# Gated attention's values turned by a round trip through DRAM and 32x32 transposes on VectorE, in place of TensorE transposes

## The chip, the cores and the metric

The kernel runs on one core of a Trainium2 chip. The time is that of one execution on the device, in microseconds (us), as the median of several runs. Five engines work side by side, each through its own list of instructions in a fixed order: TensorE (PE: matmuls, and transposes done as matmuls against an identity matrix), VectorE (DVE), ScalarE (ACT), GpSimd (POOL) and SyncE (SP, which here only starts transfers). An instruction waits on semaphores for those whose results or buffers it needs, and everything behind it on its engine waits with it. Matmul results go to PSUM, which has eight banks; all other tiles lie in SBUF.

## The reference

One decoder layer works on 256 tokens with 16 learned tokens put in front (272), at a model width of 2048, batch 1:

```
xn = rmsnorm(h);  proj = xn @ w_in
o_fox = forgetting_attention(...)            # 8 heads of width 128
g = log_sigmoid(ga @ w_alpha2 + b_alpha) / 16
o_gla = gated_linear_attention(gq, gk, gv, g) # 4 heads, keys 256, values 512 wide
o_gla = head_rmsnorm(o_gla) * silu(gr)
y = sigmoid(gate_fox) * (o_fox @ w_o_fox) + sigmoid(gate_gla) * (o_gla @ w_o_gla)
h = h + y @ w_out
h = h + squared_relu(rmsnorm(h) @ w_ff1) @ w_ff2
out = rmsnorm(h)[16:]
```

In gated linear attention every token's query and key are scaled by running products of the gates ("decay"); scores are the products of scaled queries and keys, masked to be causal, and a head's output is scores times values. The change concerns the four heads of this part alone.

## The kernel before, in words

Activations stay transposed: features on the 128 partitions, tokens on the free axis. All projections stream the weight matrices once, as chunks of 128 output columns. `next_weights` fetches a chunk as two halves of 512 KB: SP starts the transfer into `raw` (5 buffers), ACT rounds it to a high part (L128), DVE subtracts to get the low part (L129), both in one of 5 `wt` buffers. A new half can only be rounded when PE has finished with the half that was five before it. A chunk is then used by one of two products:

- `gemm2` (L144, L145): 32 matmuls on 256 tokens, its two column halves added later by `total` (ACT copies one half to `evb`, L170; DVE adds, `evt`, L173);
- `gemm_all` (L161 to L163): 48 matmuls on all 272 tokens.

Each such product writes one bank of the pool `pg`, which has three. So the fourth product from any given one needs the bank that this one filled, and can begin only when the engine that reads that result is done with it. Small results go through a pool `px` of five banks.

`later(n, fn)` puts a function aside until n more products have been issued. On top of that a scheduler settles each engine's order when the program is built; what runs in which order is fixed from then on.

A head of gated attention (`gla_head`) makes two key products (results scaled on DVE into `ki`, L511), two query products (L514), four value products, then four products for the output gate (`sg`). Head 0 has its queries and gates from earlier. Value product i is scaled by DVE into `vT` (first 256 tokens, L558) and `vE` (last 16, L559); with L559 the PSUM bank is free again. Since this gives values with features on partitions, and the output product wants tokens there, `turn` (L544 to L553) turns them: eight 128x128 TensorE transposes of `vT` and one of `vE` (L548 to L550), then the first 128 tokens are split into a high and a low part (`v0`, ACT L177 and DVE L178), the second 128 copied to `v1` (ACT L552), the last 16 to `v2` (ACT L553).

`scores` (L530) makes the masked scores `at0`, `at1`, `at2`. `outputs` multiplies them with the values into two `po` banks: twelve matmuls for the first block (L190 to L192), then those of the second (L574) and the last block (L575). ACT copies the result to `oT` (L576) and squares it into `so` (L577), POOL adds squares. `sums` adds over features (L585), and DVE forms the reciprocal root (L206 to L212). `scale` multiplies `oT` by it (L591) and by the gate (L593) and splits it (L178, into `og`). `decays` makes the gate products of the next head from DVE's scans (L436), with twelve ACT exponentials (L445, L451).

These steps of one head run among the products of the next: the root and the scaling of head 0 stand on DVE between the value products of head 1.

Of the kernel before, what the change touches and what calls it, by code (L numbers as in the profile page):

```python
# [7 lines left out]
F32 = mybir.dt.float32  # L8
# [4 lines left out]
ALU = mybir.AluOpType  # L13
# [3 lines left out]
P = 128  # L17
D = 2048
KT = D // P
NM = 16  # L20
NT = 256
# [3 lines left out]
GLA_H, GLA_DK, GLA_DV = 4, 256, 512  # L25
# [8 lines left out]
BIG = 3.0e38  # L34
RAW = 5
NL = 4

O_FQ, O_FK, O_FV, O_FF = 0, 1024, 2048, 3072
O_GQ, O_GK, O_GV, O_GR = 3080, 4104, 5128, 7176
# [29 lines left out]
def trunk(ctx: ExitStack, tc: tile.TileContext, hT, w_small, w_all, consts, w_alpha2, out):  # L69
    nc = tc.nc  # L70
    serial = [0]

    def nm(s):
        serial[0] += 1
        return f"{s}_{serial[0]}"
# [5 lines left out]
    dram = ctx.enter_context(tc.tile_pool(name="dram", bufs=1, space=bass.MemoryType.DRAM))  # L81
    pg = ctx.enter_context(tc.tile_pool(name="pg", bufs=3, space=PSUM))
    px = ctx.enter_context(tc.tile_pool(name="px", bufs=5, space=PSUM))
# [3 lines left out]
    def bank(pool, s):  # L87
        return pool.tile([P, 512], F32, tag="bank", name=nm(s))
# [5 lines left out]
    def later(n, fn):  # L94
        waiting.append([n, fn])
# [80 lines left out]
    def split_to(dst_hi, dst_lo, src):  # L176
        nc.scalar.copy(dst_hi, src)  # L177
        nc.vector.tensor_tensor(dst_lo, src, dst_hi.bitcast(F32), op=ALU.subtract)  # L178

    def split(pool, tag, src, bufs=None):  # L180

        kw = {} if bufs is None else {"bufs": bufs}
        hi = pool.tile(list(src.shape), F32R, tag=tag + "h", name=nm(tag + "h"), **kw)
        lo = pool.tile(list(src.shape), F32R, tag=tag + "l", name=nm(tag + "l"), **kw)
        split_to(hi, lo, src)
        return hi, lo

    def three(out, lhs, rhs, first, last):

        nc.tensor.matmul(out, lhs[0], rhs[0], start=first, stop=False)  # L190
        nc.tensor.matmul(out, lhs[0], rhs[1], start=False, stop=False)
        nc.tensor.matmul(out, lhs[1], rhs[0], start=False, stop=last)  # L192
# [60 lines left out]
    ident, scan = cons[:, 0:P], cons[:, P : P + NA]  # L253
# [79 lines left out]
    for s in range(KT // 2):  # L333
# [4 lines left out]
        for kk in range(2):  # L338
# [11 lines left out]
            st, sp = k == 0, k == KT - 1  # L350
            for c, (hi, lo) in enumerate(at):
                ps = first_ps[c]
# [5 lines left out]
            for c, (hi, lo) in enumerate(at):  # L358
                ps = first_ps[c]
# [28 lines left out]
    rb = keep.tile([P, NA], F32, tag="rb", name="rb")  # L388
# [113 lines left out]
    def gla_head(hd, sg, ready=None):  # L502

        ki = att.tile([P, 2, NA], F32, tag="ki", name=nm("ki"))
        q0 = ready[0] if ready else att.tile([P, 2, NT], F32, tag="qd", name=nm("qd"))
        q1 = att.tile([P, 2, NT - G1], F32, tag="q1", name=nm("q1"))
        q2 = att.tile([P, 2, NM], F32, tag="q2", name=nm("q2"))
        k2 = att.tile([P, 2, 4, NM], F32, tag="k2", name=nm("k2"))
        for i in range(2):
            ps = ready[1] if ready and i == 0 else gemm_all(next_weights(), x)  # L510
            nc.vector.tensor_tensor(ki[:, i, :], ps[:, 0:NA], rb, op=ALU.mult)  # L511
        for i in range(2):
            t = q0[:, i, :] if ready else total(gemm2(next_weights(), xt))
            nc.vector.scalar_tensor_tensor(q0[:, i, :], t, GLA_DK ** -0.5, rbt, op0=ALU.mult, op1=ALU.mult)  # L514
        e = decay[hd]
        nc.vector.tensor_tensor(ki, ki, e[:, :, Q:], op=ALU.mult)
        nc.vector.tensor_copy(k2, ki[:, :, 2 * P :].unsqueeze(2).to_broadcast([P, 2, 4, NM]))
        nc.vector.tensor_tensor(q1, q0[:, :, G1:], e[:, :, NT : Q - NM], op=ALU.mult)
        nc.vector.tensor_tensor(q2, q0[:, :, G2:], e[:, :, Q - NM : Q], op=ALU.mult)
        nc.vector.tensor_tensor(q0, q0, e[:, :, 0:NT], op=ALU.mult)  # L520

        at1 = att.tile([P, NT - G1], F32, tag="at1", name=nm("at1"))

        def scores():
            pa = bank(px, "pa")
            p0, p1, p2 = pa[:, 0:NT], pa[:, NT : 2 * NT - G1], pa[0 : 4 * NM, 2 * NT - G1 : Q]
            for dst, k, q in ((p0, ki[:, :, 0:P], q0), (p1, ki[:, :, P : 2 * P], q1),
                              (p2, k2.rearrange("p a j s -> p a (j s)"), q2)):
                for a in range(2):
                    nc.tensor.matmul(dst, k[:, a, :], q[:, a, :], start=(a == 0), stop=(a == 1))  # L530
            nc.scalar.copy(at0, p0)
            nc.scalar.copy(at1, p1)
            nc.vector.tensor_tensor(at2[0 : 4 * NM].rearrange("p (j q) -> p j q", q=NM),
                                    p2.unsqueeze(1).to_broadcast([4 * NM, 4, NM]),
                                    diag[0 : 4 * NM].rearrange("p (j q) -> p j q", q=NM), op=ALU.mult)
            for ap, n, base in ((at0[:, 0:G1], G1, NM), (at1[:, 0:P], P, 0)):
                nc.gpsimd.affine_select(ap, ap, pattern=[[1, n]], compare_op=ALU.is_ge, fill=0.0, base=base,
                                        channel_multiplier=-1)

        v1 = att.tile([P, GLA_DV], F32, tag="v1", name=nm("v1"))  # L540
        vT = att.tile([P, 4, 2 * P], F32, tag="vT", name=nm("vT"))
        vE = att.tile([P, 4 * NM], F32, tag="vE", name=nm("vE"))

        def turn():  # L544
            pv = [bank(px, n) for n in ("p0", "p1", "p2")]
            for i in range(4):
                cols = slice(P * i, P * (i + 1))
                nc.tensor.transpose(pv[0][:, cols], vT[:, i, 0:P], ident)  # L548
                nc.tensor.transpose(pv[1][:, cols], vT[:, i, P : 2 * P], ident)
            nc.tensor.transpose(pv[2][0 : 4 * NM, 0:P], vE, ident)  # L550
            split_to(*v0, pv[0])
            nc.scalar.copy(v1, pv[1])  # L552
            nc.scalar.copy(v2[0 : 4 * NM], pv[2][0 : 4 * NM, 0:P])  # L553

        later(5, scores)
        for i in range(4):
            ps = gemm_all(next_weights(), x)
            nc.vector.tensor_tensor(vT[:, i, :], ps[:, 0 : 2 * P], rb[:, 0 : 2 * P], op=ALU.mult)  # L558
            nc.vector.tensor_tensor(vE[:, NM * i : NM * (i + 1)], ps[:, 2 * P : NA], rb[:, 2 * P :], op=ALU.mult)  # L559
        later(1, turn)  # L560

        oT = att.tile([P, 4, NT], F32, tag="oT", name=nm("oT"))
        st = {}

        def outputs():
            a0 = split(att, "a0", at0)
            so = st["so"] = att.tile([P, 4, NT], F32, tag="vT", name=nm("so"))
            po = [bank(px, "po").rearrange("p (j t) -> p j t", t=NT) for _ in range(2)]
            for c in range(4):
                three(po[c // 2][:, c % 2, :], [e[:, P * c : P * (c + 1)] for e in v0], a0, c % 2 == 0, False)  # L570
            for i, pj in enumerate(po):
                for j in range(2):
                    v = slice(P * (2 * i + j), P * (2 * i + j + 1))
                    nc.tensor.matmul(pj[:, j, G1:], v1[:, v], at1, start=False, stop=False)  # L574
                nc.tensor.matmul(pj[:, :, G2:], v2, at2[:, 2 * NM * i : 2 * NM * (i + 1)], start=False, stop=True)  # L575
                nc.scalar.copy(oT[:, 2 * i : 2 * i + 2, :], pj)  # L576
                nc.scalar.activation(so[:, 2 * i : 2 * i + 2, :], pj, AF.Square)  # L577
            nc.gpsimd.tensor_tensor(so[:, 0:2, :], so[:, 0:2, :], so[:, 2:4, :], op=ALU.add)
            nc.gpsimd.tensor_tensor(so[:, 0, :], so[:, 0, :], so[:, 1, :], op=ALU.add)
            st["sq"] = split(att, "sq", so[:, 0, :])  # L580

        def sums():
            pr = bank(px, "pr")[:, 0:NT]
            for i in range(2):
                nc.tensor.matmul(pr, ones_r, st["sq"][i], start=(i == 0), stop=(i == 1))  # L585
            st["y"] = root(pr, NT, 1.0 / GLA_DV, [st["so"][:, i, :] for i in (1, 2, 3, 3)])

        def scale():
            for i in range(4):
                j = 4 * hd + i  # L590
                nc.vector.scalar_tensor_tensor(oT[:, i, :], oT[:, i, :], ggn[:, j : j + 1], st["y"], op0=ALU.mult,  # L591
                                               op1=ALU.mult)
                nc.vector.tensor_tensor(oT[:, i, :], oT[:, i, :], st["sg"][:, i, :], op=ALU.mult)  # L593
                split_to(og_tile()[j][:, 0, :], og_tile()[j][:, 1, :], oT[:, i, :])

        later(2, outputs)
        later(3, sums)
        if sg is None:
            sg = gla_gates(None)
            st["sg"] = sg  # L600
            scale()
        else:
            st["sg"] = sg
            later(8, scale)

    att = cum.enter_context(tc.tile_pool(name="att", bufs=1, reuse_waits="tile"))

# [375 lines left out]
```

## Time and profile before

| | |
|---|---|
| median of 3 runs | 1597.83 us (1597.78 to 1598.25) |
| profiled execution | 1597.77 us |
| its span, first to last instruction | 1595.8 us |
| mean granted TensorE clock | 0.998 of full speed |
| PE busy | 1585.7 us (99%) |
| DVE busy | 1056.4 us (66%) |
| ACT busy | 778.6 us (49%) |
| POOL busy | 90.4 us (6%) |
| DMA | 293.15 MB, mean 184 GB/s |

Busy times are sums over the whole span, and an engine that is busy for two thirds of it can still be late at one place. A timeline row gives start and length; matmuls and most other instructions overlap a little with their successors, so the pitch from one start to the next is what an instruction costs in a row of its kind. "Idle before" with an arrow names what ended the wait.

Gated attention's value products of head 0 lie at about 60 to 83 us, those of head 1 at about 115 to 138 us.

### The profile page before, as it was taken

The page shows a single profiled execution, that of the slowest core. Times are in us where ns is not written, and L with a number is a line of the kernel's source. Part 1 is how long each engine was busy: PE and PEld are TensorE (multiplying, and loading weights), DVE is VectorE, ACT ScalarE, POOL GpSimd, SP SyncE. Part 2 cuts the span into 40 slices and gives each one's busy share as a digit, 9 for nine tenths or more (in the row PEclk, how much of TensorE's full clock was granted, in tenths as well). Part 3 has the DMA queues.
Part 4 walks back from the last instruction along what each step waited for, and adds up shares of the span by engine and source line. Part 5 has one row for each costly group of instructions (what it writes and reads, how often), then busy time and mean ns, then how long its engine had stood idle before and what let it go on. Part 6 is the DMA issues. An engine that isn't in the chain of part 4 may idle for free.

```text
span 1595.8 us, 25249 instructions
## 1 busy us (share of the span) xinstructions
PE 1585.7 (99%) x9838; PEld 1437.4 (90%) x9838; DVE 1056.4 (66%) x1613; ACT 778.6 (49%) x1173; POOL 90.4 (6%) x139
## 2 busy tenths in 40 slices
PE   9999999999999999999999999999999999999997
PEld 8999999999998888888888888888888888888887
DVE  7777757675556666666777776667655776567655
ACT  7776444454445444444555444344433443344553
POOL 0000000011100000000011000000000000000011
PEclk9999999999999999999999999999999999999999
DMA  9444545455545555555555555555555555555552
GB/s 319 168 151 162 179 158 182 156 179 166 166 160 183 188 193 187 188 194 188 182 200 189 183 194 188 192 189 187 192 189 191 191 186 195 188 190 192 186 185 94
DMA packets 88392, 293.15 MB, mean 184 GB/s; under 512 B 9344, under 2 KB 18320, under 8 KB 88272
## 3 DMA queue, kind: packets, MB, share of 16 engines
q1 hardware_dynamic: 87104, 289.67, 54.2%
q0 software_dynamic: 448, 1.13, 0.4%
q8 instruction: 77, 1.26, 0.3%
q10 hardware_dynamic: 720, 0.74, 0.2%
q14 instruction: 43, 0.35, 0.1%
HBM read 289.39 MB, written 2.11 MB: 183 GB/s over the span
## 4 chain that ended last, share of the span: by engine, by line
PE 99%; DVE 0%; DMA 0%; ACT 0%; issue 0%; DVEq 0%; ACTq 0%
PE ps L144 50%; PE ps L145 27%; PE psa L163 5%; PE psa L162 5%; PE psa L161 5%; PE ps L354 1%; PE ps L876 1%; PE ps L361 1%; PE ps L863 0%; PE pa L530 0%; PE po L574 0%; PE psa L616 0%; DMA h<-hT_dram 0%; DVE scaled L908 0%; PE pq L683 0%; PE p L548 0%
## 5 line engine op out<-in xcount | busy, mean ns | idle before, releaser
L129 DVE TENSOR_TENSOR wt<-raw,wt 128x1024 fp32r<-128x1024 f32 x522 | 644.7, 1235 | 338.4 <-ACT wt L128 332.8
L128 ACT CAST wt<-raw 128x1024 fp32r<-128x1024 f32 x522 | 548.7, 1052 | 509.1 <-PE ps L145 277.4
L144 PE MATMUL ps<-x,wt 128*128 128x512 f32 x1952 | 680.5, 391 | 0.0
L145 PE MATMUL ps<-x,wt 128*128 128x256 f32 x1952 | 550.5, 282 | 0.0
L144 PEld LDWEIGHTS ps<-x,wt 128*128 128x128 f32 x1952 | 366.4, 188 | 75.8
L145 PEld LDWEIGHTS ps<-x,wt 128*128 128x128 f32 x1952 | 368.9, 189 | 0.2
L144 PE MATMUL ps<-a,wt 128*128 128x512 f32 x960 | 333.0, 390 | 0.0
L145 PE MATMUL ps<-a,wt 128*128 128x256 f32 x960 | 270.7, 282 | 0.0
L144 PEld LDWEIGHTS ps<-a,wt 128*128 128x128 f32 x960 | 180.1, 188 | 37.8
L161 PE MATMUL psa<-x,wt 128*128 128x272 f32 x624 | 181.7, 291 | 0.0
L145 PEld LDWEIGHTS ps<-a,wt 128*128 128x128 f32 x960 | 181.4, 189 | 0.0
L163 PE MATMUL psa<-x,wt 128*128 128x272 f32 x624 | 180.7, 290 | 0.0
L162 PE MATMUL psa<-x,wt 128*128 128x272 f32 x624 | 180.5, 289 | 0.0
L170 ACT COPY evb<-ps 128x256 f32<-128x256 f32 x160 | 59.4, 372 | 229.1 <-PE ps L145 227.2
L173 DVE TENSOR_TENSOR evt<-ps,evb 128x256 f32<-128x256 f32 x158 | 67.0, 425 | 99.0 <-ACT evb L170 98.8
L161 PEld LDWEIGHTS psa<-x,wt 128*128 128x128 f32 x624 | 117.2, 188 | 0.4
L162 PEld LDWEIGHTS psa<-x,wt 128*128 128x128 f32 x624 | 117.3, 188 | 0.0
L163 PEld LDWEIGHTS psa<-x,wt 128*128 128x128 f32 x624 | 117.2, 188 | 0.0
L144 PE MATMUL ps<-og,wt 128*128 128x512 f32 x256 | 89.2, 390 | 0.0
L144 PE MATMUL ps<-y,wt 128*128 128x512 f32 x256 | 88.8, 390 | 0.0
L145 PE MATMUL ps<-og,wt 128*128 128x256 f32 x256 | 72.2, 282 | 0.0
L145 PE MATMUL ps<-y,wt 128*128 128x256 f32 x256 | 72.2, 282 | 0.0
(281 smaller groups left out, 1317.9 us busy)
## 6 DMA issues: line engine op xcount, KB each, us to landing
raw<-w_all_dram SPq DMA_DIRECT2D x537, 512.0 KB, 3.6
raw<-w_all_dram SPq DMA_DIRECT2D x7, 384.0 KB, 5.7
h<-hT_dram SPq DMA_DIRECT2D x7, 275.0 KB, 6.1
out_dram<-scaled SPq DMA_DIRECT2D x5, 256.0 KB, 2.7
negc<-fdram POOLq DMA_DIRECT2D x8, 136.0 KB, 3.6
raw<-w_all_dram SPq DMA_DIRECT2D x2, 256.0 KB, 3.7
raw<-w_all_dram SPq DMA_DIRECT2D x2, 192.0 KB, 4.5
room<-w_small_dram SPq DMA_DIRECT2D x1, 320.0 KB, 6.4
```

What stands on the lines that cost most here:

```text
L128: nc.scalar.copy(hi[:, k, :], r)
L129: nc.vector.tensor_tensor(lo[:, k, :], r, hi[:, k, :].bitcast(F32), op=ALU.subtract)
L144: nc.tensor.matmul(ps, hi, x, start=first, stop=False)
L145: nc.tensor.matmul(ps[:, 0:NT], lo, x[:, 0, :], start=False, stop=last)
L161: nc.tensor.matmul(ps[:, 0:n], hi, x[:, k, 0, :], start=(k == 0), stop=False)
L162: nc.tensor.matmul(ps[:, 0:n], lo, x[:, k, 0, :], start=False, stop=False)
L163: nc.tensor.matmul(ps[:, 0:n], hi, x[:, k, 1, :], start=False, stop=(k == KT - 1))
L170: nc.scalar.copy(b, ps[:, NT:512])
L173: nc.vector.tensor_tensor(t, ps[:, 0:NT], b, op=ALU.add)
L354: nc.tensor.matmul(ps, hi, x[:, k, :, NM:NA], start=st, stop=False)
L361: nc.tensor.matmul(ps[:, 0:NT], lo, x[:, k, 0, NM:NA], start=False, stop=sp)
L876: pin(nc.tensor.matmul(ps[:, NT:], w(k)[0], a[k][:, :, tok], start=(k == 0), stop=(k == KT - 1)))
```

## The change

The eight TensorE transposes of `vT` per head go. `vT` is stored as 8 blocks of 32 tokens, each with the four value products side by side. `turn` sends it to a DRAM tile `rows` by one transfer (256 pieces of 2 KB), fetches it back by four transfers into `moved` (each fills 32 partitions, pieces of 512 B), and DVE then transposes it in 32x32 blocks with eight instructions of 128x128, four into `turned` and four into `v1`. All five transfers are started by POOL. `v0` is split from `turned`. ACT's copy to `v1` goes. The small transpose of `vE` stays on PE, as `turn_end`, called in `outputs` behind the twelve matmuls. `turn` is called directly behind the four value products instead of one product later; `outputs` and `sums` are each put aside one product longer, `scale` one less for heads 1 to 3. `moved` and `oT` share a buffer, and so do `vT`, `turned` and `so`. Over the program PE has 32 transposes fewer, POOL 20 transfers more, DVE 32 transposes more, ACT 4 copies fewer.

```diff
-        vT = att.tile([P, 4, 2 * P], F32, tag="vT", name=nm("vT"))
+        vT = att.tile([P, 8, 4, SQ], F32, tag="vT", name=nm("vT"))
...
         def turn():
-            pv = [bank(px, n) for n in ("p0", "p1", "p2")]
-            for i in range(4):
-                cols = slice(P * i, P * (i + 1))
-                nc.tensor.transpose(pv[0][:, cols], vT[:, i, 0:P], ident)
-                nc.tensor.transpose(pv[1][:, cols], vT[:, i, P : 2 * P], ident)
-            nc.tensor.transpose(pv[2][0 : 4 * NM, 0:P], vE, ident)
-            split_to(*v0, pv[0])
-            nc.scalar.copy(v1, pv[1])
-            nc.scalar.copy(v2[0 : 4 * NM], pv[2][0 : 4 * NM, 0:P])
+            rows = dram.tile([2 * P, 4 * P], F32, tag="rows", name=nm("rows"), bufs=2)
+            nc.gpsimd.dma_start(rows.rearrange("(g p) e -> p g e", p=P), vT.rearrange("p (g j) c s -> p g (j c s)", j=4))
+            moved = att.tile([P, 2, 4, 4, SQ], F32, tag="oT", name=nm("moved"))
+            src = rows.rearrange("(b d) (j e) -> j d b e", d=SQ, e=P)
+            for j in range(4):
+                nc.gpsimd.dma_start(moved[SQ * j : SQ * (j + 1)].rearrange("p g i c s -> p (g i) (c s)"), src[j])
+            turned = att.tile([P, GLA_DV], F32, tag="vT", name=nm("turned"))
+            for g, dst in ((0, turned), (1, v1)):
+                for c in range(4):
+                    nc.vector.transpose(dst[:, P * c : P * (c + 1)], moved[:, g, :, c, :])
+            split_to(*v0, turned)
+
+        def turn_end():
+            pv = bank(px, "p2")
+            nc.tensor.transpose(pv[0 : 4 * NM, 0:P], vE, ident)
+            nc.scalar.copy(v2[0 : 4 * NM], pv[0 : 4 * NM, 0:P])
...
-            nc.vector.tensor_tensor(vT[:, i, :], ps[:, 0 : 2 * P], rb[:, 0 : 2 * P], op=ALU.mult)
+            nc.vector.tensor_tensor(vT[:, :, i, :], ps[:, 0 : 2 * P].rearrange("p (j s) -> p j s", s=SQ),
+                                    rb[:, 0 : 2 * P].rearrange("p (j s) -> p j s", s=SQ), op=ALU.mult)
...
-        later(1, turn)
+        turn()
...
-        oT = att.tile([P, 4, NT], F32, tag="oT", name=nm("oT"))
         def outputs():
+            oT = st["oT"] = att.tile([P, 4, NT], F32, tag="oT", name=nm("oT"))
...
+            turn_end()
...
-        later(2, outputs)
-        later(3, sums)
+        later(3, outputs)
+        later(4, sums)
...
-            later(8, scale)
+            later(7, scale)
```

The new file is one line longer ahead of these functions, so the lines of products and casts read one higher there (L128 is L129, L129 is L130, L161 is L162, L177 is L178), and inside `gla_head` more (L558 is L566, L559 is L568, L591 is L602, L593 is L604, L576 is L586).

The first place where instructions move is the output of head 0, on PE. `po` are its two banks; `ps_1231` before and `ps_1197` now are the same product, the first for the queries of head 1. Before, where three of its sixteen steps have been issued:

```order
L144 MATMUL ps_1231<-x,wt_1222 128x512
L145 MATMUL ps_1231<-x,wt_1222 128x256
L144 MATMUL ps_1231<-x,wt_1222 128x512
L145 MATMUL ps_1231<-x,wt_1222 128x256
L190 MATMUL po_1190<-a0h_1185,v0h 128x256
```

And now:

```order
L145 MATMUL ps_1197<-x,wt_1193 128x512
L146 MATMUL ps_1197<-x,wt_1193 128x256
L191 MATMUL po_1236<-a0h_1231,v0h 128x256
L192 MATMUL po_1236<-a0l_1232,v0h 128x256
L193 MATMUL po_1236<-a0h_1231,v0l 128x256
```

The `po` matmuls moved behind the other 26 matmuls of that product. In front of them PE has lost the eight transposes of the head.

On ACT, at the same place, the copies of that output (`oT`, `so`) stand ahead of the twelve exponentials before:

```order
L433 ACTIVATE room<-room 128x544
L576 COPY oT_1002<-po_1190 128x512
L577 ACTIVATE so_1189<-po_1190 128x512
L576 COPY oT_1002<-po_1191 128x512
L577 ACTIVATE so_1189<-po_1191 128x512
L451 ACTIVATE decay_502<-room,ref_1168 128x128 x4
L451 ACTIVATE decay_502<-room,ref_1168 128x16 x2
L445 ACTIVATE decay_502<-room,neg_1169 128x256 x2
L445 ACTIVATE decay_502<-room,neg_1169 128x144 x2
L445 ACTIVATE decay_502<-room,neg_1169 128x16 x2
L128 CAST wt_1347<-raw_1346 128x8x128
```

and behind them now:

```order
L171 COPY evb_1269<-ps_1197 128x256
L129 CAST wt_1438<-raw_1437 128x8x128
L561 COPY v_510<-p_137_1250 64x128
L452 ACTIVATE decay_502<-room,ref_1169 128x128 x4
L452 ACTIVATE decay_502<-room,ref_1169 128x16 x2
L446 ACTIVATE decay_502<-room,neg_1170 128x256 x2
L446 ACTIVATE decay_502<-room,neg_1170 128x144 x2
L446 ACTIVATE decay_502<-room,neg_1170 128x16 x2
L586 COPY oT_1230<-po_1236 128x512
L587 ACTIVATE so_1235<-po_1236 128x512
L586 COPY oT_1230<-po_1237 128x512
L587 ACTIVATE so_1235<-po_1237 128x512
```

The four copies moved behind the twelve exponentials, which themselves wait for DVE's scans (L437).

The second place is the scaling of head 0's output on DVE, between the value products of head 1. `psa_1351` before and `psa_1356` now are the first of the four value products, `psa_1442` and `psa_1447` the second; `wt_1648` before is the second half of the chunk behind the value products, and `wt_1727` now the first half of the chunk behind that. Before:

```order
L591 SCALAR_TENSOR_TENSOR oT_1002<-oT_1002,cons,so_1189 128x256 x4
L593 TENSOR_TENSOR oT_1002<-oT_1002,sg_604 128x256
L129 TENSOR_TENSOR wt_1648<-raw_1647,wt_1648 128x8x128
L593 TENSOR_TENSOR oT_1002<-oT_1002,sg_604 128x256 x2
L558 TENSOR_TENSOR vT_1339<-psa_1351,rb 128x256
L559 TENSOR_TENSOR vE_1340<-psa_1351,rb 128x16
```

And now:

```order
L130 TENSOR_TENSOR wt_1727<-raw_1726,wt_1727 128x8x128
L602 SCALAR_TENSOR_TENSOR oT_1230<-oT_1230,cons,so_1235 128x256 x4
L534 TENSOR_TENSOR at_506<-pa_1707,corners 64x64
L179 TENSOR_TENSOR a0l_1821<-at_505,a0h_1820 128x256
L604 TENSOR_TENSOR oT_1230<-oT_1230,sg_604 128x256 x3
L566 TENSOR_TENSOR vT_1344<-psa_1356,rb 128x8x32
L568 TENSOR_TENSOR vE_1345<-psa_1356,rb 128x16
```

The release of the first value product's bank (L559, now L568) has one more weight half (`wt_1727`), and the small product and the split of head 1's scores (L534, L179), ahead of it. On PE the fourth value product of head 1 is `psa_1594` now; with three banks it takes that of `psa_1356`, and its first matmul stands directly behind the matmuls of the scores (`pa_1707`).

## Rows read from the trace of the kernel before

**Rows 1.** The page, part 1: busy time, share of the span and count of PE.
```profile
PE 1585.7 (99%) x9838; PEld 1437.4 (90%) x9838; DVE 1056.4 (66%) x1613; ACT 778.6 (49%) x1173; POOL 90.4 (6%) x139
```
**Rows 2.** Busy time by windows: length, then PE, PEld, DVE, ACT, POOL, PEclk, DMA.
```profile
60.00:335.00 275.00, 275.00 (x1961) 261.69 (x1960) 202.77 (x361) 153.58 (x257) 16.75 (x32) 1.00 0.50 166
```
**Rows 3.** Timeline of PE, head 0: start, length, line, output and inputs.
```profile
92.98 0.27 PE L549 MATMUL p<-cons,vT 128*128 128x128 f32 x1
...
93.64 0.27 PE L549 MATMUL p<-cons,vT 128*128 128x128 f32 x1
...
97.93 0.28 PE L190 MATMUL po<-a0h,v0h 128*128 128x256 f32 x1
```
**Rows 4.** Timeline of PE, head 1: its scores, fourth value product, and a gate product.
```profile
129.33 1.03 PE L530 MATMUL pa<-qd,ki 128*128 128x256 f32 x4
...
131.34 0.37 PE L161 MATMUL psa<-x,wt 128*128 128x272 f32 x1
...
143.67 0.48 PE L144 MATMUL ps<-x,wt 128*128 128x512 f32 x1
...
149.30 0.28 PE L190 MATMUL po<-a0h,v0h 128*128 128x256 f32 x1
```
**Rows 5.** Timeline of DVE, head 1, up to the release of the first value product.
```profile
126.95 1.67 DVE L591 SCALAR_TENSOR_TENSOR oT<-oT,cons,so 128x256 f32<-128x256 f32 x4
...
128.87 1.22 DVE L129 TENSOR_TENSOR wt<-raw,wt 128x1024 fp32r<-128x1024 f32 x1
130.01 0.76 DVE L593 TENSOR_TENSOR oT<-oT,sg 128x256 f32<-128x256 f32 x2
130.68 0.42 DVE L558 TENSOR_TENSOR vT<-psa,rb 128x256 f32<-128x256 f32 x1
131.01 0.17 DVE L559 TENSOR_TENSOR vE<-psa,rb 128x16 f32<-128x16 f32 x1
```
**Rows 6.** Timeline of ACT, head 0: output copies, exponentials, a cast.
```profile
100.14 0.59 ACT L576 COPY oT<-po 128x512 f32<-128x512 f32 x1
...
103.70 1.68 ACT L451 ACTIVATE decay<-room,ref 128x128 f32<-128x128 f32 x6 [1.50 <-DVE ref L440]
105.29 1.90 ACT L445 ACTIVATE decay<-room,neg 128x256 f32<-128x256 f32 x6
107.10 1.04 ACT L128 CAST wt<-raw 128x1024 fp32r<-128x1024 f32 x1
```
**Rows 7.** Timeline of DVE, head 0: last value release, the splits of its weights, the scans.
```profile
82.94 0.16 DVE L559 TENSOR_TENSOR vE<-psa,rb 128x16 f32<-128x16 f32 x1
...
90.87 2.41 DVE L129 TENSOR_TENSOR wt<-raw,wt 128x1024 fp32r<-128x1024 f32 x2 [2.21 <-ACT wt L128]
...
100.99 1.34 DVE L436 TENSOR_TENSOR_SCAN room<-ones,room 128x272 f32<-128x272 f32 x2
```
**Rows 8.** DMA issues: output and input, queue, count, KB each, median us to landing.
```profile
raw<-w_all_dram SPq DMA_DIRECT2D x537, 512.0 KB, 3.6
...
negc<-fdram POOLq DMA_DIRECT2D x8, 136.0 KB, 3.6
...
fdram<-room POOLq DMA_DIRECT2D x1, 8.5 KB, 3.8
```
**Rows 9.** Timeline of POOL in forgetting attention: a stretched copy and a DMA issue.
```profile
333.13 1.08 POOL L673 COPY nc<-negc 128x16 f32<-128x16 f32 x1 [0.39 <-DMA negc<-fdram]
...
340.00 0.56 POOL L652 DMA_DIRECT2D negc<-fdram  x1 [5.05 <-DVE st L688]
343.75 0.19 POOL L673 COPY nc<-negc 128x16 f32<-128x16 f32 x1 [3.20 <-DMA negc<-fdram]
```
**Rows 10.** Timeline of DVE beside that DMA issue.
```profile
339.62 1.22 DVE L129 TENSOR_TENSOR wt<-raw,wt 128x1024 fp32r<-128x1024 f32 x1
```
**Rows 11.** Timeline of PE at the start of the program.
```profile
1.28 4.18 PE L328 MATMUL warm<-ones 128*128 128x256 f32 x10 [1.28 <-DVE cons L252]
```
**Rows 12.** Busy time by windows behind the last matmul; columns as in rows 2.
```profile
1590.00:1595.80 5.80, 0.00 (x0) 0.00 (x0) 1.24 (x3) 0.00 (x0) 0.00 (x0) 0.50 0.55 174
```

More of the change, by code (lines that the diff above doesn't have):

```diff
@@ L36 @@
 NL = 4
+SQ = 32
 O_FQ, O_FK, O_FV, O_FF = 0, 1024, 2048, 3072
@@ L588, in scale @@
         def scale():
+            oT = st["oT"]
             for i in range(4):
```

## The prediction

> **What bounds the kernel now.** I read the busy times first: PE is busy for 99% of the span [rows 1], DVE for 66%, ACT for 49%, POOL for 6%. In the whole stretch in which the four heads run, 60 to 335 us, PE is busy for 275.00 of 275.00 us at a granted clock of 1.00 [rows 2]. So there what PE no longer has to do is gained in full, what the other engines do more costs nothing as long as PE waits for none of it, and any wait of PE's is loss. The question is therefore whether the work that moves to DMA and DVE stays in time for PE. For that I followed in the timelines what PE needs in heads 0 and 1: the turned values, and a free PSUM bank.
>
> **What is removed.** The transposes of a head follow each other at a pitch of (93.64 - 92.98)/6 = 0.11 us [rows 3]. 32 of them go: 32 x 0.11 = 3.5 us of PE. The small transpose now stands between products of another kind, which may cost a few hundredths per head: 0.1 in all. Net -3.4 us. ACT loses four 512-wide copies of 0.6 each [rows 6], nothing that PE waits for.
>
> **The round trip.** Last value of head 0 to last landing of `moved`, called D. The trace has no such transfer. The write moves 512 KB to DRAM through POOL's queue: from below, a weight half of the same size lands after 3.6 us, from above add the 3.8 us of the only small DRAM write [rows 8], 7.4; I take 5.0, nearer to the row with the same bytes. The four reads are issued one after the other: three issues at 0.56 [rows 9], 1.7 us until the last, or twice that if an issue of 256 pieces takes double; the last lands 3.6 later, as `negc` on the same queue [rows 8]. D is 5.0 + 1.7 + 3.6, with hand-overs 10.5; bounds 8.9 and 14.5.
>
> The last value of head 0 is done at 83.1, so `moved` is there at 93.6. DVE's list has the eight transposes right behind the two weight splits that end at 93.3 [rows 7], so D up to 10.2 stops nobody. A 128x128 block transpose does not occur before; its price lies between the 0.17 of a narrow instruction and the 0.42 of a two-input one of 256 columns [rows 5]; I take 0.3, eight are 2.4 us. The Trainium skill, page "VectorE: DVE Perf Modes", section "The three transpose paths", gives 311 ns for such a transpose of 16-bit values; no run here shows it, and with it the eight would be 2.5 us. Behind them, up to the sum `evt` that the next step needs, DVE has two weight splits at a pitch of 130.01 - 128.87 = 1.14 and some 3,100 columns of smaller work at 0.33 us per 256 columns (130.68 to 131.01) [rows 5]: 2.3 + 4.1, so it is there at 93.6 + 2.4 + 6.4 = 102.4, against 102.0 when PE and ACT have that sum's inputs (next part). That is 0.4 late, and beyond it each microsecond of D is one more on DVE. PE needs `v0` at 101.6; DVE has it some 4 us earlier, so PE itself waits for values only if D is above some 14.
>
> **The wait that is new.** The outputs of head 0 move behind 26 more of the 32 matmuls of a product. Such a product takes 149.30 - 143.67 = 5.6 us [rows 4], so they start at 97.93 [rows 3] + 4.6 - 0.9 (eight transposes) = 101.6. More important is what ACT does then: its four copies of the output now stand behind the twelve exponentials, and these wait for DVE's scans, which now come behind `evt`. The chain: product ready 101.6, `evb` 0.4, `evt` 0.4 (102.4, or 102.8 by the late DVE), scans 1.3 [rows 7], the query scaling 0.3, a split 1.1, three narrow ones 0.3: 105.8. Exponentials 107.10 - 103.70 = 3.4; the four copies 103.70 - 1.50 - 100.14 = 2.1; the cast behind them 1.0 [rows 6]: 112.3. Before, the copies were over at 102.2.
>
> From there DVE's list has no gap up to the instruction that releases the PSUM bank of head 1's first value product (L568): 8 weight splits x 1.14 = 9.1; 18 two-input instructions of 256 columns x 0.33 = 5.9; the four L602 1.6 (128.87 - 126.95 less one of 0.33); scans 1.3; the smaller rest some 2,500 columns, 3.3 [rows 5, 7]. Together 21.2: 133.5.
>
> A second route ends at the same release and does not depend on D. `wt_1727` stands ahead of it now, and its buffer comes free only when PE has finished the third value product, 129.33 [rows 4] - 0.9 = 128.4. From there cast 1.0 [rows 6], split 1.2, four L602 1.6, the two score instructions 0.5, three L604 1.0, then L566 and L568 0.5 [rows 5]: 134.2, with hand-overs 134.6.
>
> PE wants the bank earlier. Before, DVE had it free at 131.18 [rows 5] and the fourth value product began at 131.34 [rows 4], so there is no reserve. Now PE comes there after the scores at 131.34 - 0.9 - 0.2 (two transposes of head 1 that stood in between) = 130.2. It waits until 134.6: 4.4 us. Bounds: 3.3 if only the first route counts, some 7 with the upper D. In heads 2 and 3 the list has the scaling ahead of the value products, and each release directly behind its product, so I charge nothing there.
>
> **The clock.** PE runs at its upper level (2.4 GHz) in all of the stretch [rows 2]. Where it has stood still behind its last matmul the granted clock is 0.50 [rows 12], the lower level, 1.2 GHz. At the start of the program, coming from rest, ten 128x256 matmuls take 4.18 us [rows 11], while four take 1.03 in the full stretch [rows 4], so ten would be 2.6: coming out of rest costs 1.6 us. Whether a wait of 4.4 us is enough for a fall no row of before shows, since PE's longest is the 1.28 of its start [rows 11]. I take that it is: 1.6 us, bounds 0 and 3.2 (twice).
> The Trainium skill, page "TensorE: Matmul & The Clock Gate", section "HAM oscillation — how this bites in real kernels", says that a kernel which waits between bursts of matmuls drops to the lower clock in the wait and runs the beginning of the next burst at half speed. By that rule the sum is the one below, without it 1.6 us less; the trace so far agrees as far as the row behind the last matmul goes.
>
> **The sum** on the profiled execution (1597.77 us, of which 1595.8 is span and 2.0 lies around it; the median of the runs, 1597.83, is the same within 0.1): 1597.77 - 3.4 + 4.4 + 1.6 = 1600.4 us.
>
> **The rivals.**
> A, the forecast: bank wait and clock fall, 1600.4; its own range with the spread of the wait, 1599.4 to 1602.
> B: the bank wait without a fall of the clock, 1597.77 - 3.4 + 4.4 = 1598.8. For it: the wait is short. Against: the granted clock behind the last matmul is at the lower level as soon as a row is without PE work.
> C, clearly slower: the round trip is long. The first route passes the second when D is above 11.6, and from there each microsecond of D is one of PE's. With an issue of 256 pieces at 1.1 instead of 0.56 and the write at 6.4, D is 6.4 + 3.4 + 3.8 = 13.6, the wait 6.4: 1602.4. At the upper bound, 14.5, it is 1603.3, and the output of each head begins to wait for `v0`.
> D, held issues: POOL instructions can be stretched beside DVE's. A copy of 16 columns took 1.08 us where the same line took 0.19 later [rows 9]. If each of the five issues loses the 0.9 of that row, D is 15.0: the bank wait grows by 3.4 and each of four heads' outputs waits 1 us, 1600.4 + 3.4 + 3 = 1607. Against it: the issue at 340.00 lay wholly within a DVE split that began at 339.62 and took 1.22 [rows 9, 10], and was over in 0.56. The Trainium skill, page "SBUF — State Buffer", section "SBUF: two separate sides", has this as a trap: transfers started by GpSimd need descriptors that it cannot write while a VectorE instruction holds the port that the two share. By that rule the time would be that of D; the row of the issue speaks against it for the splits, which are most of DVE's work, and says nothing of DVE's one-input instructions.
> E, the whole gain: DVE is earlier than I count, the bank is free in time and PE loses nothing: 1594.4. It needs the second route to be 4 us shorter, and four of its six terms are rows of the same instructions.
>
> **Chances.** A 0.50, B 0.20, C 0.18, D 0.06, E 0.06. The prediction is A's 1600.4. The range 1598.2 to 1604.5 holds A, B and C and leaves out D and E. A measurement of this kernel can tell some 0.2%, 3.2 us, from no change: faster is below 1594.6, slower above 1601.0. Faster: half of E and a little for what I did not see, 0.06. Slower: three tenths of A (0.15), all of C and D, 0.39, rounded to 0.40. Same: the rest, 0.54.
>
> **What would show it.** In the profile of the changed kernel: a wait of PE of 4 to 5 us ahead of the fourth value product of head 1 (L162), near 130 to 135 us, released by DVE's L568, and no other wait of PE above half a microsecond in 60 to 335 us. In a window right behind it a granted clock well below 1.00 (A), or 1.00 (B). The copies L586 of head 0 behind the exponentials, over near 111. `rows` and `moved` landing with 5 and 3.6 us, POOL's issues near 0.56; block transposes near 0.3. The prediction is wrong if PE waits for `v0` in L191 (C, D), if the value product of head 1 begins at 130 without a wait (E), or if the waits are in other heads, where I charged none.

## The result, and the profile after

The changed kernel takes 1604.04 us (median of 6 runs, 1603.72 to 1604.58) against 1597.9 for the kernel before in the same rounds: 6.1 us slower, a ratio of 1.0039 with a 95% interval of 1.0029 to 1.0050. Its profiled execution took 1604.08 us, its span 1602.4, so I compare its trace with [rows 1 to 12] directly.

The list of PE's waits over the whole program, in total, times and longest:

```profile
PE psa L162 <- ACT og L178: 6.5, 1, 6.5
PE warm L329 <- DVE cons L253: 1.3, 1, 1.3
PE pn L907 <- ACT sq L892: 0.8, 1, 0.8
PE pn L914 <- DVE ry L812: 0.3, 1, 0.3
PE ps L887 <- DVE h L875: 0.3, 1, 0.3
PE po L193 <- DVE v0l L179: 0.3, 1, 0.3
```

One wait is new and large: 6.5 us ahead of a value product. PE's timeline shows which, the fourth of head 1, directly behind the scores, where before it began without a wait [rows 4]:

```profile
130.33 0.41 PE L531 MATMUL pa<-q,k 128*64 128x16 f32 x4
137.23 0.57 PE L162 MATMUL psa<-x,wt 128*128 128x272 f32 x1 [6.49 <-ACT og L178]
137.59 0.43 PE L163 MATMUL psa<-x,wt 128*128 128x272 f32 x1
...
141.38 0.29 PE L162 MATMUL psa<-x,wt 128*128 128x272 f32 x1
141.51 0.29 PE L163 MATMUL psa<-x,wt 128*128 128x272 f32 x1
```

The list names ACT's cast of `og` as the releaser, but that is only the event that ended nearest: this product reads nothing of `og`. The bank comes free with DVE's L568, which ends at 137.08 (DVE's timeline, answering to [rows 5]):

```profile
132.28 1.29 DVE L130 TENSOR_TENSOR wt<-raw,wt 128x1024 fp32r<-128x1024 f32 x1
133.50 1.69 DVE L602 SCALAR_TENSOR_TENSOR oT<-oT,cons,so 128x256 f32<-128x256 f32 x4
135.12 0.20 DVE L534 TENSOR_TENSOR at<-pa,corners 64x64 f32<-64x64 f32 x1
...
136.59 0.41 DVE L566 TENSOR_TENSOR vT<-psa,rb 128x256 f32<-128x256 f32 x1
136.93 0.15 DVE L568 TENSOR_TENSOR vE<-psa,rb 128x16 f32<-128x16 f32 x1
```

The clock fell in the wait. In the windows of this stretch (length; busy time and count of PE, PEld, DVE, ACT and POOL; granted clock, DMA share, GB/s) it is still 1.00 where PE has just stopped, and 0.50, the 1.2 GHz level, when the product begins:

```profile
131.00:134.00 3.00, 0.00 (x0) 0.00 (x0) 3.00 (x5) 1.51 (x4) 1.73 (x2) 1.00 0.25 82
134.00:137.00 3.00, 0.00 (x0) 0.00 (x0) 3.00 (x11) 0.97 (x3) 0.00 (x0) 0.58 0.71 246
137.00:141.00 4.00, 3.77 (x17) 3.81 (x18) 2.58 (x10) 0.51 (x2) 0.00 (x0) 0.50 0.04 16
141.00:145.00 4.00, 4.00 (x32) 4.00 (x32) 1.23 (x1) 1.05 (x1) 0.00 (x0) 0.96 0.00 0
```

From 137.23 to 141.38 PE starts 18 matmuls of 272 columns. At the full clock they follow each other at 0.125 us (141.38 to 141.51 is such a step), so they would take 2.25; they took 4.15. The fall costs 1.9 us.

How DVE came to be so late is seen upstream. POOL's timeline and the transfers' landing in head 0 (issue to landing, median) give the round trip:

```profile
83.14 0.76 POOL L547 DMA_DIRECT2D rows<-vT  x1 [6.12 <-DVE vE L568]
87.05 2.38 POOL L551 DMA_DIRECT2D moved<-rows  x4 [3.15 <-DMA rows<-vT]
```
```profile
rows<-vT POOLq DMA_DIRECT2D x1, 512.0 KB, 3.6
moved<-rows POOLq DMA_DIRECT2D x4, 128.0 KB, 7.9
```

And on DVE and ACT, what it holds up (answering to [rows 6, 7]):

```profile
90.69 2.41 DVE L130 TENSOR_TENSOR wt<-raw,wt 128x1024 fp32r<-128x1024 f32 x2 [2.21 <-ACT wt L129]
96.89 0.89 DVE L555 STREAM_TRANSPOSE turned<-moved 128x128 f32<-128x128 f32 x4 [3.79 <-DMA moved<-rows]
97.71 0.85 DVE L555 STREAM_TRANSPOSE v<-moved 128x128 f32<-128x128 f32 x4
...
104.70 0.41 DVE L174 TENSOR_TENSOR evt<-ps,evb 128x256 f32<-128x256 f32 x1
...
114.37 1.49 DVE L130 TENSOR_TENSOR wt<-raw,wt 128x1024 fp32r<-128x1024 f32 x1 [6.20 <-ACT wt L129]
```
```profile
107.99 1.68 ACT L452 ACTIVATE decay<-room,ref 128x128 f32<-128x128 f32 x6 [4.14 <-DVE ref L441]
109.57 1.90 ACT L446 ACTIVATE decay<-room,neg 128x256 f32<-128x256 f32 x6
...
112.80 0.59 ACT L587 ACTIVATE so<-po 128x512 f32<-128x512 f32 x1
113.29 1.04 ACT L129 CAST wt<-raw 128x1024 fp32r<-128x1024 f32 x1
```

The values were done at 82.9 and `moved` was there at 96.9: a trip of 14.0 us, the last read 7.9 of it (over the four heads the median read took 6.3). DVE stood still for 3.8 us before the transposes, reached `evt` at 104.7, and ACT waited 4.1 us for DVE's scans with the four finished copies and the next weight cast queued behind the exponentials. Then it was DVE's turn to wait, 6.2 us for that cast.

### The profile page after: what moved, and what is told of

It reads as the page before. It is cut to its first block, busy times and chain, and to the rows that moved or that the text cites. A ratio compares the mean times of both kernels' runs of the same rounds, so it can differ in the third digit from the quotient of the medians.

```text
span 1602.4 us, 25251 instructions
## 1 busy us (share of the span) xinstructions
PE 1585.8 (99%) x9806; PEld 1436.3 (90%) x9806; DVE 1060.9 (66%) x1645; ACT 775.5 (48%) x1169; POOL 106.6 (7%) x159
## 4 chain that ended last, share of the span: by engine, by line
PE 93%; issue 2%; DVE 2%; DMA 1%; POOL 1%; ACT 0%; DVEq 0%; POOLq 0%; ACTq 0%
PE ps L145 49%; PE ps L146 26%; PE psa L163 4%; PE psa L162 4%; PE psa L164 4%; PE ps L355 1%; DMA moved<-rows 1%; PE ps L887 1%; PE ps L362 1%; DMA rows<-vT 0%; DVE wt L130 0%; PE ps L874 0%; PE warm L329 0%; PE psa L627 0%; POOL moved L551 0%
## 5 line engine op out<-in xcount | busy, mean ns | idle before, releaser
L130 DVE TENSOR_TENSOR wt<-raw,wt 128x1024 fp32r<-128x1024 f32 x522 | 646.3, 1238 | 331.4 <-ACT wt L129 326.4
L129 ACT CAST wt<-raw 128x1024 fp32r<-128x1024 f32 x522 | 548.5, 1052 | 499.9 <-PE ps L146 274.4
L162 PE MATMUL psa<-x,wt 128*128 128x272 f32 x624 | 182.4, 292 | 6.5 <-ACT og L178 6.5
L162 PEld LDWEIGHTS psa<-x,wt 128*128 128x128 f32 x624 | 118.1, 189 | 7.1 <-ACT og L178 6.6
L797 POOL TENSOR_TENSOR acc<-acc,hsq 128x256 f32<-128x256 f32 x26 | 27.8, 1068 | 769.0 <-ACT hsq L796 769.0
```

The lines of the kernel that those rows point to most:

```text
L129: nc.scalar.copy(hi[:, k, :], r)
L130: nc.vector.tensor_tensor(lo[:, k, :], r, hi[:, k, :].bitcast(F32), op=ALU.subtract)
L162: nc.tensor.matmul(ps[:, 0:n], hi, x[:, k, 0, :], start=(k == 0), stop=False)
L797: nc.gpsimd.tensor_tensor(acc, acc, sq, op=ALU.add)
```

## The experiments

The theory: the loss is the wait for the bank in head 1 and the clock that falls in it, made by the order of the copies behind the exponentials and lengthened by the trip. The rivals: the round trip itself costs (its transfers against the weight stream, its transposes on DVE); or the order alone, without the trip; or what is gained and lost comes from elsewhere. Medians stand beside those of the kernel before, run in the same rounds; single runs of one kernel differ by more than 4 us where PE waits, so waits and clocks are read from the traces, each of which shows one execution.

**Four banks.** The changed kernel with

```diff
-    pg = ctx.enter_context(tc.tile_pool(name="pg", bufs=3, space=PSUM))
-    px = ctx.enter_context(tc.tile_pool(name="px", bufs=5, space=PSUM))
+    pg = ctx.enter_context(tc.tile_pool(name="pg", bufs=4, space=PSUM))
+    px = ctx.enter_context(tc.tile_pool(name="px", bufs=4, space=PSUM))
```

> The changed kernel with four PSUM banks for the big products instead of three (and four for the small ones instead of five). Theory (the loss is PE's wait for the bank of head 1's first value product, and the clock that falls in it): the fourth value product starts at about 130.8 us without a wait, the product behind it may wait up to 1 us for the same release near 137.5, the granted clock stays at 1.00; 1604.0 - 6.5 - 2.0 + 0.9 = 1596.4 us, below the kernel before. Rival (the loss lies in the round trip itself, its transfers and what they do to DVE, POOL and the weight stream): the wait only moves, and the time stays above 1601.

1597.39 us (before 1597.95; ratio 0.9997, 0.9988 to 1.0006), profiled execution 1596.58; the median is 1.0 above what was expected, and the runs spread from 1596.46 to 1598.78. From PE's waits and the window behind:

```profile
PE ps L145 <- ACT og L178: 1.1, 1, 1.1
```
```profile
137.00:141.00 4.00, 3.23 (x19) 2.90 (x20) 4.00 (x14) 1.54 (x6) 1.26 (x3) 1.00 0.70 240
```

The 6.5 us are gone, the product behind waits 1.1 us for the same release, and the clock stays at 1.00. The trip and the transposes are still there, so the rival that they cost by themselves falls: the loss of 6 us was the bank and the clock.

**The counts alone.** The kernel before, TensorE transposes and all, with

```diff
-        later(2, outputs)
-        later(3, sums)
+        later(3, outputs)
+        later(4, sums)
...
-            later(8, scale)
+            later(7, scale)
```

> The kernel before with nothing but the three counts of the change (outputs and sums of a head one product later, scaling one earlier); the TensorE transposes stay, no round trip. Theory (the late release has two parts: the order that the counts give, and the long round trip behind it): the output copies stand behind the exponentials here too, but DVE reaches them about 2.3 us earlier than in the changed kernel, so PE waits some 3 us for the bank in head 1; whether the clock falls is open: 1601 without, 1603 with a fall. Rival (the round trip alone makes the wait): no wait above 0.5 us, 1598.2 (switches of the outputs a few tenths).

1600.90 us (ratio 1.0017, 1.0008 to 1.0026). PE waits here too, for the same instructions of DVE, but stops one place earlier, at the first transpose of head 1, which needs `vT`:

```profile
133.84 0.33 PE L548 MATMUL p<-cons,vT 128*128 128x128 f32 x1 [2.27 <-DVE vT L558]
```
```profile
134.00:137.00 3.00, 3.00 (x16) 3.00 (x16) 2.83 (x11) 1.26 (x5) 0.00 (x0) 0.55 0.48 162
```

2.3 us of wait and a fallen clock without any round trip: the order alone makes nearly half of the loss. The expected 3 us of wait were 0.7 too many, and the time with a fall was expected at 1603. Six of the eleven spans lie at 1599.2 to 1599.7 us, the traced one (1599.5) among them, and five at 1597.4 to 1598.3. That would fit a clock that falls in some of the executions only, since the fall is worth nearly 2 us, but the shorter ones were not traced.

**No round trip.** The changed kernel with the transposes reading the values where they lie:

```diff
-            rows = dram.tile([2 * P, 4 * P], F32, tag="rows", name=nm("rows"), bufs=2)
...
-                nc.gpsimd.dma_start(moved[SQ * j : SQ * (j + 1)].rearrange("p g i c s -> p (g i) (c s)"), src[j])
-            turned = att.tile([P, GLA_DV], F32, tag="vT", name=nm("turned"))
+            moved = vT.rearrange("p (g j) c s -> p g j c s", j=4)
+            turned = att.tile([P, GLA_DV], F32, tag="oT", name=nm("turned"))
```

> The changed kernel without the round trip: the block transposes read the scaled values where they lie (so their 32x32 blocks stay in the wrong places and the outputs of gated attention are not those of the reference); everything else stays. Theory: DVE is some 2.3 us earlier at the scans, the copies are over near 111 instead of 113.4, the release comes near 134.8 and PE waits 4 us instead of 6.5: 1601.5 with a fall of the clock, 1599.5 without. Rival (order alone): the wait stays above 6 and the time at 1604. Rival (round trip alone): no wait, 1595.5.

The values stay in the wrong places here, so this version serves for the time alone. It takes 1601.13 us (ratio 1.0018, 1.0009 to 1.0027); PE waits 4.83 us (4 expected), until 135.58, and the clock falls. DVE's timeline ahead of the release:

```profile
130.17 1.23 DVE L130 TENSOR_TENSOR wt<-raw,wt 128x1024 fp32r<-128x1024 f32 x1 [0.52 <-ACT wt L129]
131.31 0.50 DVE L213 SCALAR_TENSOR_TENSOR so<-so 128x256 f32<-128x256 f32 x1
...
132.34 1.67 DVE L597 SCALAR_TENSOR_TENSOR oT<-oT,cons,so 128x256 f32<-128x256 f32 x4
...
135.27 0.16 DVE L563 TENSOR_TENSOR vE<-psa,rb 128x16 f32<-128x16 f32 x1
```

This is the second route of the prediction, seen alone: DVE now waits 0.5 us for the cast of the half that was `wt_1727`, begun at 129.09, right behind the end of the third value product (129.06), and from the split to the release it is 5.3 us of listed work. The trip was worth 1.7 us of the 6.5, not all and not nothing; both pure rivals fall.

**Gate products later.** The changed kernel with

```diff
-        later(1 + 3 * hd, lambda hd=hd: with_table(decays, hd))
-    later(3 * GLA_H - 1, lambda: with_table(forget))
+        later((1, 4, 9, 13)[hd], lambda hd=hd: with_table(decays, hd))
+    later(14, lambda: with_table(forget))
```

> The changed kernel with the gate products of heads 2 and 3 (scans and exponentials) put aside two and three products longer, which nothing needs before heads 2 and 3. The output copies of head 0 then stand ahead of the exponentials again. Theory: the first route to the release is cut by some 5 us, the second one (the weight half wt_1727 ahead of the release, whose buffer comes free with the third value product) decides, near 133; PE waits about 2.3 us, the clock stays: 1604.0 - 6.5 - 2.0 + 2.3 = 1597.8 us. Rival (the second route does not count): no wait, 1595.5. Rival (the exponentials have nothing to do with it): 1604.

1601.73 us (ratio 1.0022, 1.0012 to 1.0032). The copies of head 0's output no longer stand behind the exponentials, and the release comes at 133.4 (rows of ACT, DVE and PE):

```profile
108.17 0.63 ACT L587 ACTIVATE so<-po 128x512 f32<-128x512 f32 x1
...
128.76 1.05 ACT L129 CAST wt<-raw 128x1024 fp32r<-128x1024 f32 x1 [1.99 <-PE psa L164]
```
```profile
130.31 1.22 DVE L130 TENSOR_TENSOR wt<-raw,wt 128x1024 fp32r<-128x1024 f32 x1
...
133.27 0.16 DVE L568 TENSOR_TENSOR vE<-psa,rb 128x16 f32<-128x16 f32 x1
```
```profile
133.58 0.56 PE L162 MATMUL psa<-x,wt 128*128 128x272 f32 x1 [2.97 <-DVE vE L568]
```

The release was expected near 133 and the wait at 2.3; it was 2.97, and the clock fell (0.53 in 134 to 137), where I had expected it to stay. With 1.5 us of waits for `v0` at the outputs of head 1 (0.9 and 0.6; 0.3 in the changed kernel), that makes most of the 3.9 us by which the time missed what was expected. What it shows for the cause: with the first route cut, most of the second is left. ACT's cast, released by the third value product, is over at 129.8, and from the split of that half (130.31) to the release it is 3.1 us. DVE took the split 0.5 after the cast, since its own list had no gap there; so the second route alone would have released the bank near 132.9.

**A control for the four banks.** The kernel before with the same two lines as the first experiment.

> The kernel before with four PSUM banks for the big products and four for the small ones, nothing else. A control for the four-bank version of the changed kernel: the kernel before has no wait for a bank in the four heads, so theory: no change, 1597.8 within 0.5 us. Rival (the four banks help by themselves, and the gain of the four-bank changed kernel is theirs): 1596.5 or less.

1597.84 us (before 1597.79; ratio 1.0001, 0.9992 to 1.0010): the four banks are worth nothing without the wait.

**Both edits.** Four banks and the later gate products, in the changed kernel.

> The changed kernel with four banks for the big products, and the gate products of heads 2 and 3 put aside longer. Theory: the 1.1 us that the four-bank version still waited for the release (near 137.5) goes, since the release comes near 133 and PE wants that bank at 136.8; the clock stays at 1.00: 1596.6 - 1.1 = 1595.5 us. Rival (with the exponentials later, another wait comes up in head 2 or at the values of head 0): 1597 or more.

1594.48 us (before 1597.79; ratio 0.9981, 0.9972 to 0.9989). PE has no wait in the four heads:

```profile
60.00:335.00 275.00, 275.00 (x1951) 261.49 (x1950) 207.12 (x391) 151.19 (x251) 29.48 (x47) 1.00 0.58 182
```

It is 1 us below what was expected; the waits for `v0` that the four-bank version still had (0.3 and 0.2 in its list) went as well, which is half of that.

**The trip through SP.** The four-bank version with `nc.sync.dma_start` in place of `nc.gpsimd.dma_start` in `turn`, for all five transfers.

> The four-bank version with the five transfers of the round trip started by SP instead of POOL. Theory (the long reads are POOL's four issues of 0.6 us and the competition of the weight stream, half and half): the trip takes 10 to 11 us instead of 14, the values are there 3 us earlier, the small waits for v0 in the heads (0.2 each) go: 1596.6 - 0.8 = 1595.8 us. Rival (the competition alone makes the reads long): the last read still lands 7 us after its issue, the trip is 12.5 us. Rival (SP, which waits for the values and for the rows, holds up the weight stream): PE waits for weights near 85 to 100 us and in the other heads, 1600 or more.

1595.03 us (ratio 0.9987, 0.9978 to 0.9996). The landing times of the reads, over the four heads:

```profile
moved<-rows SPq DMA_DIRECT2D x16, 128.0 KB, 3.3
```

The same reads land after 3.3 instead of 5.9 us in the version that starts them from POOL, and `moved` is there 10.2 us after the last value (84.56 to 94.76). The time is 0.8 below what was expected, and the rival of held-up weights falls, since PE waits for none. But the pair does not tell POOL's queue from competition, because the weight stream is not the same. SP starts the weights too, and it stands still while it waits for `rows`. In head 3 (first SP's list, then the windows in which the reads start, with SP and with POOL):

```profile
287.00 0.33 SPq L127 DMA_DIRECT2D raw<-w_all_dram  x1
291.18 1.81 SPq L551 DMA_DIRECT2D moved<-rows  x4
293.09 10.15 SPq L127 DMA_DIRECT2D raw<-w_all_dram  x4
```
```profile
291.00:293.00 2.00, 2.00 (x16) 1.70 (x15) 0.46 (x2) 1.44 (x4) 0.52 (x2) 1.00 0.35 108
```
```profile
292.00:294.00 2.00, 2.00 (x16) 1.70 (x15) 1.91 (x4) 1.46 (x4) 1.47 (x3) 1.00 0.74 254
```

From 287.3 to 293.1 no weight half is started, so the reads start with the DMA engines busy for 0.35 of the window instead of 0.74. In head 0, the one that decides, both versions load them alike (busy share 0.76 to 1.01 in every 2 us from 84 to 94), and there the reads take nearly the same, with POOL and with SP:

```profile
moved<-rows POOLq DMA_DIRECT2D x4, 128.0 KB, 5.4
```
```profile
moved<-rows SPq DMA_DIRECT2D x4, 128.0 KB, 5.3
```

The trip of head 0 is 11.2 us with POOL and four banks (84.98 to 96.17), only 1.0 longer than with SP. So what made the reads long, the queue or the load, stays open. POOL's own issues took 0.59 each in the changed kernel (9.4 us for 16) and were never stretched. The Trainium skill, page "SBUF — State Buffer", section "SBUF: two separate sides", advises ACT's or SP's queue for such transfers, on the ground that certain VectorE instructions keep GpSimd from writing the descriptors. The version with SP is the faster of the pair (1595.0 against 1597.4 us); issues held by VectorE are not what the trace shows.

**The trip through SP, three banks.** The changed kernel with that edit alone, so that the trip has the length that the prediction took.

> The changed kernel, with its three banks, and the five transfers started by SP. This puts the trip at about the 10.5 us that the prediction took, and leaves the rest of its sum as it stood. Theory (the prediction's chain was right and the length of the trip was the term that was off): PE waits 4 to 5 us for the bank in head 1 instead of 6.5, the clock falls and costs 2, the small waits for the values go: 1604.0 - 2.0 - 0.9 = 1601.1 us. Rival (the wait does not hang on the trip): 6 us or more, 1603.

1602.15 us (ratio 1.0025, 1.0016 to 1.0034), its profiled execution 1600.42, the fastest of its runs:

```profile
134.93 0.37 PE L162 MATMUL psa<-x,wt 128*128 128x272 f32 x1 [4.22 <-DVE vE L568]
```
```profile
93.84 0.89 DVE L555 STREAM_TRANSPOSE turned<-moved 128x128 f32<-128x128 f32 x4 [5.00 <-DMA moved<-rows]
```

The trip takes 10.6 us, PE waits 4.2, the clock falls. So the wait does hang on the trip, though the median is 1.1 above what was expected. The scheduler also put the split of the scores behind the release here, worth some 0.3 of it. The prediction's sum, 1600.4, is met by the execution whose trace is shown, but this is the fastest of ten; the median lies 1.7 higher.

**All three.** Four banks, later gate products, the trip through SP.

> The changed kernel with four banks for the big products, the gate products of heads 2 and 3 put aside longer, and the transfers started by SP. Theory: PE waits for nothing in the four heads, so the full 3.2 us of the TensorE transposes are gained and no more: 1597.8 - 3.2 = 1594.6 us, the same as the four-bank version with later gate products (1594.5). Rival (that version still loses something to the long trip): 1593.8 or less.

1594.75 us (before 1597.95; ratio 0.9980, 0.9971 to 0.9989), the same as with the trip through POOL: once PE waits for nothing, a shorter trip brings nothing.

**A control for both edits.** The kernel before with four banks and later gate products.

> A control: the kernel before with four banks and the later gate products, TensorE transposes kept. Theory: PE waits for nothing before and nothing here, 1597.8 within 0.5. Rival (the gain of the version of the changed kernel with the same two edits is that of the edits, not of the transposes): 1595.

1597.52 us (ratio 0.9997, 0.9988 to 1.0006). So the 3.2 us of the two versions above are those of the transposes, and not of the edits that let them through (2.8 against this control, whose own 0.4 lies within its interval).

## Why the prediction was right or wrong, point by point

The direction, the place and the mechanism were right, and the time lies in the range, near its upper end; but it is nearer to rival C's than to A's: 1602.4 to 1603.3 was forecast there, 1604.0 measured. So it is slower by more than the 0.2% that I could tell, for which I had given 0.40, against 0.54 for no change. C's own terms, a longer issue and a slower write, did not come; it was the reads that were long.

- **The gain** was right: -3.4 forecast. The version in which PE waits for nothing gains 1597.95 - 1594.75 = 3.2.
- **The new wait** was at the place named, released by the instruction named, and it is the only one above half a microsecond in the heads. Its size was off: 4.4 forecast, 6.5 measured. ACT's copies of head 0's output were over at 113.4, near 111 forecast.
- **The step that failed is the length of the trip**, and in it one term: "the last lands 3.6 later, as `negc` on the same queue". The last read of head 0 landed after 7.9. The write was shorter (3.6, taken as 5.0) and the issues were near (0.59, taken as 0.56). So D was 14.0, not 10.5, within its bounds of 8.9 and 14.5. By the prediction's own rule, one for one above 11.6, a D of 14.0 gives a wait of 6.8; measured 6.5. With D at 10.6 (the trip through SP, three banks) the wait was 4.2.
- **Luck in the first route.** That the rule comes so near is in part luck, for two terms missed by some 1.5 us each and cancelled. With 3.5 more of D the cast behind the copies would be over at 112.3 + 3.5 = 115.8; it was over at 114.3. From there DVE's list was counted at 21.2 and took 22.7 (114.37 to 137.08).
- **The second route** was right in kind: a release at 134.6 whatever the trip does. Without a trip it came at 135.4. PE also came to the bank later, at 130.7 instead of 130.2.
- **The clock** fell as assumed and cost 1.9, forecast 1.6. The Trainium skill's rule ("TensorE: Matmul & The Clock Gate", "HAM oscillation — how this bites in real kernels") agrees: 0.50 where the product begins. The price was taken from the start of the program, where the profile's windows show no fallen clock (1.00 from 0 to 6 us). So it is not shown that the two have the same cause, and the nearness of the price may be luck.
- **Small waits** were charged at nothing and cost about 0.9: 6.1 measured is -3.2 + 6.5 + 1.9 and 0.9 more. Only 0.3 of it is in the list (`v0l` in head 1). The rest is a remainder and was not traced. Places like these two matmuls of head 2's output, 0.26 apart where others of the kind are 0.11, may hold some of it:

```profile
236.90 0.28 PE L192 MATMUL po<-a0l,v0h 128*128 128x256 f32 x1
237.16 0.39 PE L193 MATMUL po<-a0h,v0l 128*128 128x256 f32 x1
```

- **The block transposes** took 0.27 each and followed each other at 0.20, so eight cost 1.6 (2.4 taken). **Held issues** (rival D) did not happen: sixteen issues at 0.59. **The whole gain** (E) needed the second route to be 4 us shorter, and it was not.

Not settled: whether POOL's queue or the load makes the reads long, and why runs of one kernel with a wait differ by more than 4 us.

## What to carry to other kernels

An engine that is busy for 99% of the time pays for a wait that the change puts into somebody else's list, so after moving work, look for the buffer that this engine needs next and follow the instruction that releases it back through both other engines' orders. A gain of 3 us was turned into a loss of 6 by one missing bank, and came back in full when there was a bank more and the gate products stood later. Take the price of a transfer from rows of the same queue only if size, direction and load agree as well, and carry the upper bound through the chain to the point from which it decides.

## What the runs showed of the hardware

- Four 128 KB reads from DRAM started by POOL landed after 5.9 to 6.6 us (the medians of the versions), started by SP after 3.2 to 3.5, but with SP less of the weight stream ran beside them. In head 0 they took 7.9 and 5.4 from POOL (three and four banks) and 5.3 from SP (four banks), so the figure is not one of the queue alone.
- Waits of PE of 2.3, 3.0, 4.2, 4.8 and 6.5 us were each followed, in the traced executions, by a granted clock of 0.50; one of 1.1 us left it at 1.00. So the price of a wait is not its length alone: 1.9 us came on top of 6.5.
- A 32x32 block transpose of 128x128 four-byte values on DVE takes 0.27 us; in a row they follow each other at 0.20, two-input instructions of 256 columns at 0.33.
